# A three-layer block in split fp32: the other feature-major projections in wide and narrow matmuls, in two banks

## The chip, the core and the metric

The kernel runs on one core of a Trainium2 chip. The metric is the time of one execution in device microseconds (us); the median over runs counts. TensorE (PE) multiplies, ScalarE (ACT) and VectorE (DVE) work on the results and prepare the weights, GpSimd (POOL) does a few small things, and SyncE (SP) starts most of the transfers. Each engine works through its own queue in the order in which the program was written, and the engines wait for each other through semaphores.

## What is computed

The reference is a transformer of three layers on 256 tokens of width 1024, in fp32. The first block has a gated convolution, a stick-breaking attention with 16 heads, a cross attention and an MLP. The second block is a hybrid layer, run twice: eight heads of attention with a forget bias ("fox"), four heads of retention, and an MLP. The projections that the change touches are these:

```python
proj = h @ w_in[l]                                       # first block
c_h, c_b, c_c, sq, sk, sv, xq, gate_pre = jnp.split(proj, split_idx, axis=-1)
y_conv = (c_b * causal_depthwise_conv(c_c * c_h, conv_w[l])) @ w_conv_out[l]
...
proj = jnp.einsum('bsd,dc->bsc', x, w_in)                # second block, per layer
fq, fk, fv, f_logit, rq, rk, rv, rg = jnp.split(proj, SPLITS, axis=-1)
...
ret_out = jax.nn.silu(rg) * ret
```

sq, sk, c_h, c_c, c_b of the first block and fq, fk, rg of the second are wanted feature-major: features in the partitions, tokens along the free dimension.

## The kernel before

**Split products.** Every fp32 operand is held as two parts, a rounded "hi" and the rest "lo". A product is three matmuls: hi by hi, hi by lo and lo by hi (`mm3`, L324). The activations lie as `xT` (L440): a tile of 128 partitions by 8 feature blocks by 2 parts by 256 tokens, so that for one feature block the hi part and the lo part stand side by side in 512 columns.

**Weights.** The weights come in chunks of 128 x 2048 (`Stream`, L166), each in two pieces. For a piece SP starts a transfer of 512 KB, ACT rounds it to hi (L213) and DVE subtracts to get lo (L214). `W.pump(1)` issues one piece, and two where fewer than three chunks are ready ahead; five chunks have buffers. `tick()` (L283) is the clock of the program: it lets every generator in `sides` go on to its next `yield`, which issues that generator's work at this place of all queues, and then pumps the weights. So the order of work on each engine is written out by where the ticks stand.

**Feature-major chunks.** `stream_a` (L370) takes a chunk of 256 output features and one accumulator, a bank of PSUM with 512 fp32. Its left half takes features 0 to 127 for 256 tokens (24 matmuls of 256 columns), then comes a `tick()`, then the right half takes the other 128 features (24 more). It returns the accumulator, and the caller reads it there: `split` (L316) rounds on ACT and subtracts on DVE; `ch` is copied by ACT; `cc` and `cb` are multiplied by DVE; `rg` goes through Silu on ACT. There are 32 such chunks: five in each of the four passes of the loop at L554 (sq, sk, ch, cc, cb), and in each of the two layers of the second block fq, fk, fq, fk (L1133) and rg, rg (L1216).

`stream_w` (L352) is the other form, which the MLPs use before the change too (36 chunks): two accumulators, one for each half of the features. Sixteen matmuls of 512 columns take the hi weights by both parts of x side by side, then comes the `tick()`, and then 16 matmuls of 256 columns add the lo weights by the hi part. The two halves of an accumulator are then added by whoever evicts it; in the MLPs that is one DVE reduction.

**Accumulators.** `acc()` (L263) takes one of four banks. A bank is given back when its last reader stands in the program, and of the free ones the one given back longest ago is handed out (so the addresses in the program before go). A tile that gets a bank must wait until the readers of the tile before it have run. The other four banks serve `aux()` and `bank()`.

**The side work of the loop at L554.** `sb_pair` (L512) is started twice in each pass, after sk. By ticks, the first pair issues its scores (12 small matmuls into an `aux`, L516) at the tick inside cc; with them, at the same place, three activations on ACT (L522 to L524) and three operations on DVE (L525 to L527). At the tick after cc it issues an exponential on ACT (L530) and a mask product on DVE (L532). At the tick inside the next pass's sq it issues six transposes on PE and a copy `pt` on ACT (L541); and at the tick after the next sk its products with v (called PV here, 8 small matmuls into an `acc()`, L546) and their split into `osb`. The second pair does the same from the tick inside the next sq: scores there, transposes after ch, and PV at the tick inside cb.

**The side work in the layers.** During fq and fk, `csum_side` and `ret_qk_side` (L1037, L1052) each use an `acc()` at a time. `ret_side` (L1162) starts at the tick inside the first rg chunk: it takes one accumulator and then two (`ps`), whose group norm on DVE and POOL (L1185 to L1191) ends with `on`. All of that stands in the queues ahead of what follows that tick.

Of the kernel before, what the change touches and what calls it, by code (L numbers as in the profile page):

```python
# [9 lines left out]
F32 = mybir.dt.float32  # L10
F32R = mybir.dt.float32r
BF16 = mybir.dt.bfloat16
AF = mybir.ActivationFunctionType
ALU = mybir.AluOpType
# [3 lines left out]
S = 256  # L18
# [221 lines left out]
def block_kernel(ctx: ExitStack, tc: tile.TileContext, a: dict, out: bass.AP, upto=None, dbg=None):  # L240
    nc = tc.nc
    ctx.enter_context(tc.manual_schedule())

    def pool(stack, name, bufs=1, side="left", space=None):
        kw = {} if space is None else {"space": space}
        return stack.enter_context(tc.tile_pool(name=name, bufs=bufs, side=side, reuse_waits="tile", **kw))
# [16 lines left out]
    def acc():  # L263
        return accp.tile([128, 512], F32, tag="acc", name="acc")
# [9 lines left out]
    def bank():  # L274
        assert cur_ps[0][1] == 1
        return cur_ps[0][0].tile([128, 512], F32, tag="bank", name="bank")
# [3 lines left out]
    W = Stream(nc, rp, wp, a["wpack"])  # L280
    sides = []

    def tick(n=1):  # L283
        for g in list(sides):
            if next(g, "end") == "end":
                sides.remove(g)
        W.pump(n)
# [17 lines left out]
    def act_set(name):  # L305
        if cur_set[0] != name:
            nc.scalar.preload_act_table_set(name)
            cur_set[0] = name

    def tt(o, x, y, op):  # L310
        nc.vector.tensor_tensor(o, x, y, op=op)

    def stt(o, x, s, y, op0, op1):
        nc.vector.scalar_tensor_tensor(out=o, in0=x, scalar=s, in1=y, op0=op0, op1=op1)  # L314

    def split(hi, lo, src):  # L316
        nc.scalar.copy(hi, src)  # L317
        tt(lo, src, hi.bitcast(F32), ALU.subtract)

    def split_scaled(hi, lo, src, s):  # L320
        nc.scalar.mul(hi, src, s)
        stt(lo, src, s, hi.bitcast(F32), ALU.mult, ALU.subtract)

    def mm3(o, lh, ll, rh, rl, first, last):  # L324
        nc.tensor.matmul(o, lhsT=lh, rhs=rh, start=first, stop=False, skip_group_check=True)  # L325
        nc.tensor.matmul(o, lhsT=lh, rhs=rl, start=False, stop=False, skip_group_check=True)  # L326
        nc.tensor.matmul(o, lhsT=ll, rhs=rh, start=False, stop=last, skip_group_check=True)  # L327
# [9 lines left out]
    def mm(o, l, r, first=True, last=True):  # L337
        nc.tensor.matmul(o, lhsT=l, rhs=r, start=first, stop=last, skip_group_check=True)  # L338

    def unit_a(o, w, nt, x):  # L340
        for k in range(8):
            ns = slice(nt * 128, nt * 128 + 128)
            mm3(o, w[0][:, k, ns], w[1][:, k, ns], x[0][:, k, :], x[1][:, k, :], k == 0, k == 7)
# [8 lines left out]
    def stream_w(key, x, evict):  # L352

        w = W.get(key)
        ps = [acc(), acc()]
        for nt in range(2):
            for k in range(8):
                mm(ps[nt].rearrange("p (s t) -> p s t", s=2), w[0][:, k, nt * 128:nt * 128 + 128], x[2][:, k],  # L360
                   k == 0, False)
        tick()
        for nt in range(2):
            for k in range(8):
                mm(ps[nt][:, 0:S], w[1][:, k, nt * 128:nt * 128 + 128], x[0][:, k, :], False, k == 7)
            if nt:
                W.free()
            evict(nt, ps[nt].rearrange("p (s t) -> p t s", s=2))

    def stream_a(key, x):  # L370
        w = W.get(key)
        p = acc()
        pv = p.rearrange("p (n t) -> p n t", n=2)
        unit_a(pv[:, 0, :], w, 0, x)
        tick()
        unit_a(pv[:, 1, :], w, 1, x)
        W.free()
        return pv

    def stream_b(key, x, evict=None):  # L380

        p = [acc(), acc()]
        for j in range(2):
            w = W.get((*key, j))
            for t in range(2):
                unit_b(p[t], w, t, x, 4 * j, j == 0, j == 1)
                if t:
                    W.free()
                if j and evict is not None:
                    evict(t, p[t])  # L390
                if not (j and t):
                    tick()
        return p
# [46 lines left out]
    def new_xT():  # L440

        xT = ap.tile([128, 8, 2, S], F32R, tag="xT", name="xT")
        return xT[:, :, 0, :], xT[:, :, 1, :], xT


    hT = new_xT()
# [49 lines left out]
    sp = pool(st1, "sb", side="right")  # L496
# [55 lines left out]
        split(osb[0][:, pair, :], osb[1][:, pair, :], o[:, 0:256])  # L552

    for i in range(4):  # L554
        p = stream_a(("sq", i), hT)
        split_scaled(qs[0], qs[1], p, 0.125)
        tick()
        p = stream_a(("sk", i), hT)
        split(kb[0], kb[1], p)
        tick()  # L560
        sides.append(sb_pair(i, 0, 2, 3))
        sides.append(sb_pair(i, 1, 6, 4))
        p = stream_a(("ch", i), hT)
        chs = sp.tile([128, 2, S], F32, tag="chs", name="chs")
        nc.scalar.copy(chs, p)
        tick()
        p = stream_a(("cc", i), hT)
        tt(u[:, :, 2:], p, chs, ALU.mult)
        cv = sp.tile([128, 2, S], F32, tag="cv", name="cv")
        for nt in range(2):  # L570
            ct = 2 * i + nt
            nc.vector.tensor_scalar(cv[:, nt, :], u[:, nt, 0:S], cw[:, ct, 0:1], None, op0=ALU.mult)
            stt(cv[:, nt, :], u[:, nt, 1:S + 1], cw[:, ct, 1:2], cv[:, nt, :], ALU.mult, ALU.add)
            stt(cv[:, nt, :], u[:, nt, 2:S + 2], cw[:, ct, 2:3], cv[:, nt, :], ALU.mult, ALU.add)
        tick()
        p = stream_a(("cb", i), hT)
        tt(cv, p, cv, ALU.mult)
        split(yc[0][:, 2 * i:2 * i + 2, :], yc[1][:, 2 * i:2 * i + 2, :], cv)
        tick()
# [45 lines left out]
    for n in range(2):  # L625
# [4 lines left out]
        def evict(t, p):  # L630
            tt(sg[:, t, :], p, sg[:, t, :], ALU.mult)
            tt(merged[:, t, ns], merged[:, t, ns], sg[:, t, :], ALU.add)
# [90 lines left out]
    for h in range(2):  # L723
        box = {}
        p = stream_b(("xk", h), memT)
# [3 lines left out]
        p = stream_b(("xq", h), hT)  # L729
        box["qn"] = qk_prep(p, gq, "q")  # L730
        tick()
        p = stream_b(("xv", h), memT)
# [241 lines left out]
    xT = x2T[0]  # L974
    for l in range(2):
        st = ExitStack()
        p2 = pool(st, f"mix{l}")

        def T(shape, dt, tag, bufs=1):
            return p2.tile(shape, dt, tag=tag, name=tag, bufs=bufs)  # L980
# [23 lines left out]
        for t in range(2):  # L1004
            pk = bank()
            for i in range(2):
                p = bank()
# [68 lines left out]
        fp = pool(fst, f"fox{l}", side="right")  # L1076
# [54 lines left out]
            split(mix[0][:, pair, :], mix[1][:, pair, :], o[:, 0:256])  # L1131

        for i in range(2):  # L1133
            p = stream_a((l, "fq", i), xT)
            split_scaled(fqs[0], fqs[1], p, 0.125)
            tick()
            p = stream_a((l, "fk", i), xT)
            split(fkb[0], fkb[1], p)
            tick()
            for nt in range(2):  # L1140
                fox.append(fox_pair(i, nt, *((0, 1, 4, 9), (0, 4, 7, 10), (1, 3, 6, 8), (4, 6, 8, 10))[2 * i + nt]))
            sides.extend(fox[-2:])
# [70 lines left out]
        rgt = T([128, 4, S], F32, "rkT")  # L1213
        ret = ret_side()
        sides.append(ret)
        for i in range(2):  # L1216
            p = stream_a((l, "rg", i), xT)
            s = rgt[:, 2 * i:2 * i + 2, :]
            act_set(SILU)
            nc.scalar.activation(s, p, AF.Silu)  # L1220
            rgs[f"s{i}"] = s
            tick()
        nT = [None]
# [71 lines left out]
        xT = nT2[0]  # L1295
# [33 lines left out]
```

## Time and profile before

| | us |
|---|---|
| median of 3 runs (1205.63 to 1205.94) | 1205.88 |
| the profiled execution | 1206.04 |
| its span, first to last instruction | 1204.3 |

| engine | busy us | share of the span |
|---|---|---|
| PE | 1192.1 | 99% |
| DVE | 783.6 | 65% |
| ACT | 631.6 | 52% |

The profile is one execution, taken instruction by instruction. A busy share is an average over all stages. The chain of waits is followed back from the last instruction: at each step to what released it, or to the instruction before it on its engine. The timeline gives start and duration of each instruction in order of time. Matmuls overlap in the pipeline, so what one costs is the distance from its start to the start of the next, and not its duration. PEclk is the clock that TensorE was granted, as a share of 2.4 GHz. The forms x8, x12 and so on count instructions that one row holds.

### The profile page before, as it was taken

What the parts mean: (1) busy time and instruction counts of PE and PEld (TensorE: products, weight loads), DVE (VectorE), ACT (ScalarE), POOL (GpSimd) and SP (SyncE); (2) the same over time, 40 slices, a digit from 0 to 9 for tenths busy, and PEclk for the clock granted to TensorE, in tenths of its full rate; (3) what the DMA queues carried; (4) which work ended last, traced back from release to release, by engine and by line L of the source; (5) the groups of instructions that cost most, each with busy time, mean ns of one, the idle gap of its engine ahead of it and who ended that gap; (6) DMA issues with size and microseconds to landing.
All of it is one profiled execution on the core that took longest, in us unless ns stands there. A gap on an engine that the chain in (4) does not pass through costs nothing.

```text
span 1204.3 us, 17150 instructions
## 1 busy us (share of the span) xinstructions
PE 1192.1 (99%) x6801; PEld 1030.6 (86%) x6801; DVE 783.6 (65%) x1018; ACT 631.6 (52%) x885; POOL 27.1 (2%) x45
## 2 busy tenths in 40 slices
PE   8999999999999999999999999999999999999997
PEld 5999997888888888888898888888889888888886
DVE  6487776566665666566576686655667668665563
ACT  6455555455554566455255556645535555664550
POOL 1000000000000000000000100000000010000000
PEclk8999999999999999999999999999999999999999
DMA  8644456765455675555544366565545436656430
GB/s 324 236 134 140 148 176 194 250 194 173 143 163 187 192 241 193 210 174 206 169 163 143 120 218 224 182 222 173 195 153 185 140 126 217 219 186 228 162 136 35
DMA packets 60608, 218.92 MB, mean 182 GB/s; under 512 B 6864, under 2 KB 7264, under 8 KB 60528
## 3 DMA queue, kind: packets, MB, share of 16 engines
q1 hardware_dynamic: 58320, 210.99, 52.3%
q0 software_dynamic: 1776, 6.38, 1.6%
q8 instruction: 53, 0.87, 0.3%
q10 hardware_dynamic: 432, 0.46, 0.1%
q14 instruction: 27, 0.22, 0.1%
HBM read 216.75 MB, written 1.05 MB: 181 GB/s over the span
## 4 chain that ended last, share of the span: by engine, by line
PE 98%; DMA 1%; DVE 0%; POOLq 0%; issue 0%; ACT 0%; DVEq 0%; SPq 0%
PE acc L338 19%; PE bank L325 13%; PE bank L326 13%; PE bank L327 13%; PE acc L325 12%; PE acc L327 12%; PE acc L326 12%; PE acc L423 2%; PE aux L334 1%; DMA raw<-in_wpack_dram 1%; DMA gmix<-in_g_mix_dram 1%; PE aux L1119 0%; PE aux L539 0%; PE aux L326 0%; PE aux L327 0%; PE aux L325 0%
## 5 line engine op out<-in xcount | busy, mean ns | idle before, releaser
L214 DVE TENSOR_TENSOR wlo<-raw,whi 128x1024 fp32r<-128x1024 f32 x392 | 465.6, 1221 | 103.0 <-ACT whi L213 99.7
L213 ACT CAST whi<-raw 128x1024 fp32r<-128x1024 f32 x392 | 394.9, 1049 | 93.9 <-PE bank L327 41.3
L325 PE MATMUL bank<-whi,hid 128*128 128x512 f32 (+1 forms) x388 | 150.6, 388 | 0.5 <-DVE x L314 0.5
L326 PE MATMUL bank<-wlo,hid 128*128 128x512 f32 (+1 forms) x388 | 150.3, 387 | 0.0
L327 PE MATMUL bank<-whi,hid 128*128 128x512 f32 (+1 forms) x388 | 150.1, 387 | 0.0
L325 PE MATMUL acc<-xT,whi 128*128 128x256 f32 x512 | 147.6, 288 | 0.0
L326 PE MATMUL acc<-xT,whi 128*128 128x256 f32 x512 | 144.8, 283 | 0.0
L327 PE MATMUL acc<-xT,wlo 128*128 128x256 f32 x512 | 144.8, 283 | 0.0
L338 PE MATMUL acc<-xT,whi 128*128 128x512 f32 x576 | 136.9, 390 | 0.0
L338 PEld LDWEIGHTS acc<-xT,whi 128*128 128x128 f32 x576 | 107.0, 188 | 21.5
L826 ACT ACTIVATE r<-r 128x512 f32<-128x512 f32 x36 | 22.8, 633 | 148.3 <-DVE r L867 148.3
L325 PEld LDWEIGHTS acc<-xT,whi 128*128 128x128 f32 x512 | 98.0, 191 | 1.9 <-issue 1.0
L326 PEld LDWEIGHTS acc<-xT,whi 128*128 128x128 f32 x512 | 98.1, 192 | 0.2
L327 PEld LDWEIGHTS acc<-xT,wlo 128*128 128x128 f32 x512 | 98.0, 191 | 0.0
L325 PE MATMUL acc<-whi,xT 128*128 128x512 f32 x224 | 90.8, 405 | 0.3 <-ACT xT L317 0.2
L326 PE MATMUL acc<-wlo,xT 128*128 128x512 f32 x224 | 88.4, 395 | 0.5 <-DVE wlo L214 0.5
L327 PE MATMUL acc<-whi,xT 128*128 128x512 f32 x224 | 88.4, 395 | 0.0
L325 PEld LDWEIGHTS bank<-whi,hid 128*128 128x128 f32 x388 | 72.9, 188 | 15.0 <-DVE x L314 0.7
L327 PEld LDWEIGHTS bank<-whi,hid 128*128 128x128 f32 x388 | 72.9, 188 | 15.0
L326 PEld LDWEIGHTS bank<-wlo,hid 128*128 128x128 f32 x388 | 73.0, 188 | 14.1
L867 DVE TENSOR_REDUCE r<-acc 128x256 f32<-128x512 f32 x72 | 48.0, 688 | 50.9 <-PE acc L338 50.9
L338 PEld LDWEIGHTS acc<-xT,wlo 128*128 128x128 f32 x576 | 73.6, 191 | 2.6
(276 smaller groups left out, 1761.0 us busy)
## 6 DMA issues: line engine op xcount, KB each, us to landing
raw<-in_wpack_dram SPq DMA_DIRECT2D x388, 512.0 KB, 4.4
raw<-in_wpack_dram SPq DMA_DIRECT2D x4, 528.0 KB, 4.1
gb<-in_ln_g_dram POOLq DMA_DIRECT2D x4, 512.0 KB, 3.9
bb<-in_ln_b_dram POOLq DMA_DIRECT2D x4, 512.0 KB, 5.5
x<-in_x_dram SPq DMA_DIRECT2D x3, 512.0 KB, 5.7
mem<-in_mem_dram SPq DMA_DIRECT2D x2, 512.0 KB, 6.5
cst<-in_c_dram POOLq DMA_DIRECT2D x1, 898.0 KB, 9.1
out_dram<-x SPq DMA_DIRECT2D x3, 256.0 KB, 2.0
```

The costliest lines, as they stand in the source:

```text
L213: nc.scalar.copy(hi, raw)
L214: nc.vector.tensor_tensor(lo, raw, hi.bitcast(F32), op=ALU.subtract)
L325: nc.tensor.matmul(o, lhsT=lh, rhs=rh, start=first, stop=False, skip_group_check=True)
L326: nc.tensor.matmul(o, lhsT=lh, rhs=rl, start=False, stop=False, skip_group_check=True)
L327: nc.tensor.matmul(o, lhsT=ll, rhs=rh, start=False, stop=last, skip_group_check=True)
L334: nc.tensor.matmul(o[:, h, :], lhsT=q[a][hs[h]], rhs=k[b][hs[h]], start=i == 0, stop=i == 2, skip_group_check=True)
L338: nc.tensor.matmul(o, lhsT=l, rhs=r, start=first, stop=last, skip_group_check=True)
L423: nc.tensor.transpose(o[:, k * 128:(k + 1) * 128], src[:, k * 128:(k + 1) * 128], ident)
L826: nc.scalar.activation(dst, src, AF.Relu)
L867: lambda nt, h: nc.vector.tensor_reduce(rv[:, nt, :], h, AX.X, ALU.add))
```

## The change

`stream_a` goes. In its place `stream_s` computes the 32 chunks with `stream_w`, and evicts each of the two accumulators into a tile in SBUF: ACT copies the first half, and DVE adds the second half to that copy. The callers then read the SBUF tile in place of the accumulator. The new tiles are called `st` (two buffers); `ch` and `rg` are evicted straight into their own tiles, and the Silu of rg runs in place. The tick inside the chunk now stands after the 16 wide matmuls.

```diff
-    def stream_a(key, x):
-        w = W.get(key)
-        p = acc()
-        pv = p.rearrange("p (n t) -> p n t", n=2)
-        unit_a(pv[:, 0, :], w, 0, x)
-        tick()
-        unit_a(pv[:, 1, :], w, 1, x)
-        W.free()
-        return pv
+    def stream_s(key, x, dst):
+
+        def evict(nt, h):
+            nc.scalar.copy(dst[:, nt, :], h[:, :, 0])
+            tt(dst[:, nt, :], h[:, :, 1], dst[:, nt, :], ALU.add)
+
+        stream_w(key, x, evict)
+        return dst
...
-        p = stream_a(("sq", i), hT)
+        p = stream_s(("sq", i), hT, sp.tile([128, 2, S], F32, tag="st", name="st", bufs=2))
         split_scaled(qs[0], qs[1], p, 0.125)
...
-        p = stream_a(("ch", i), hT)
-        chs = sp.tile([128, 2, S], F32, tag="chs", name="chs")
-        nc.scalar.copy(chs, p)
+        chs = stream_s(("ch", i), hT, sp.tile([128, 2, S], F32, tag="chs", name="chs"))
...
-            p = stream_a((l, "rg", i), xT)
-            s = rgt[:, 2 * i:2 * i + 2, :]
+            s = stream_s((l, "rg", i), xT, rgt[:, 2 * i:2 * i + 2, :])
             act_set(SILU)
-            nc.scalar.activation(s, p, AF.Silu)
+            nc.scalar.activation(s, s, AF.Silu)
```

sk, cc, cb, fq and fk change as sq does. `stream_w`, which is not changed, is the function that it now calls:

```python
w = W.get(key)
ps = [acc(), acc()]
for nt in range(2):
    for k in range(8):
        mm(ps[nt].rearrange("p (s t) -> p s t", s=2), w[0][:, k, nt * 128:nt * 128 + 128], x[2][:, k], k == 0, False)
tick()
for nt in range(2):
    for k in range(8):
        mm(ps[nt][:, 0:S], w[1][:, k, nt * 128:nt * 128 + 128], x[0][:, k, :], False, k == 7)
    if nt:
        W.free()
    evict(nt, ps[nt].rearrange("p (s t) -> p t s", s=2))
```

## Rows read from the trace of the kernel before

**Rows 1.** Page, part 1: engine, busy us (share of span), instructions.
```profile
PE 1192.1 (99%) x6801; PEld 1030.6 (86%) x6801; DVE 783.6 (65%) x1018; ACT 631.6 (52%) x885; POOL 27.1 (2%) x45
```

**Rows 2.** Page, part 4: chain that ended last, by engine.
```profile
PE 98%; DMA 1%; DVE 0%; POOLq 0%; issue 0%; ACT 0%; DVEq 0%; SPq 0%
```

**Rows 3.** Waits of PE: waiter, releaser, us in total, times, longest.
```profile
PE acc L423 <- DVE ht L314: 2.2, 1, 2.2
PE acc L325 <- ACT xT L317: 0.2, 1, 0.2
```

**Rows 4.** Timeline of PE: start, duration in us, line, output<-inputs, shape.
```profile
37.02 0.28 PE L325 MATMUL acc<-xT,whi 128*128 128x256 f32 x1
57.26 0.51 PE L334 MATMUL aux<-kb,q 64*128 64x256 f32 x4
```

**Rows 5.** Chain in order of time (start, us, what), two MLP stretches.
```profile
447.41 1.92 PE acc L338 x16
460.24 11.11 PE acc L338 x64
```

**Rows 6.** The same chain, 56 to 160 us: scores of the attention pairs.
```profile
57.33 0.84 PE aux L334 x12
104.67 0.84 PE aux L334 x12
114.32 0.81 PE acc L338 x8
124.60 0.84 PE aux L334 x12
158.72 0.84 PE aux L334 x12
```

**Rows 7.** Timeline of ACT, third iteration of the head loop.
```profile
107.53 0.79 ACT L541 COPY pt<-aux 128x768 f32<-128x768 f32 x1
117.23 0.58 ACT L317 CAST kb<-acc 128x512 fp32r<-128x512 f32 x1
125.53 0.81 ACT L522 ACTIVATE e<-aux 128x768 f32<-128x768 f32 x1 [2.01 <-PE aux L334]
128.00 1.03 ACT L213 CAST whi<-raw 128x1024 fp32r<-128x1024 f32 x1
131.91 0.85 ACT L530 ACTIVATE r<-r 128x768 f32<-128x768 f32 x1 [2.87 <-DVE r L311]
133.59 0.36 ACT L317 CAST osbh<-acc 128x256 fp32r<-128x256 f32 x1
```

**Rows 8.** Timeline of DVE, the same iteration.
```profile
115.62 0.68 DVE L314 SCALAR_TENSOR_TENSOR q<-acc,q 128x512 fp32r<-128x512 f32 x1
119.09 0.68 DVE L311 TENSOR_TENSOR kb<-acc,kb 128x512 fp32r<-128x512 f32 x1
128.13 0.96 DVE L314 SCALAR_TENSOR_TENSOR e<-aux,e 128x768 f32<-128x768 f32 x1 [3.35 <-ACT e L524]
131.79 1.22 DVE L214 TENSOR_TENSOR wlo<-raw,whi 128x1024 fp32r<-128x1024 f32 x1
132.92 0.68 DVE L311 TENSOR_TENSOR u<-acc,chs 128x512 f32<-128x512 f32 x1
136.25 0.68 DVE L311 TENSOR_TENSOR r<-r,dmask 128x512 f32<-128x512 f32 x1
137.99 0.42 DVE L311 TENSOR_TENSOR osbl<-acc,osbh 128x256 fp32r<-128x256 f32 x1
139.46 0.68 DVE L311 TENSOR_TENSOR cv<-acc,cv 128x512 f32<-128x512 f32 x1
```

**Rows 9.** Timeline, first layer of the second block: PE, then DVE.
```profile
674.30 0.28 PE L325 MATMUL acc<-xT,whi 128*128 128x256 f32 x1
677.26 0.88 PE L338 MATMUL acc<-fpt,ta 128*64 128x256 f32 x8
682.27 0.36 PE L325 MATMUL acc<-xT,whi 128*128 128x256 f32 x1
692.73 0.48 PE L325 MATMUL bank<-whi,mixh 128*128 128x512 f32 x1
680.77 0.30 DVE L1185 BATCH_NORM_STATS2 gst<-acc 128x6 f32<-128x128 f32 x1 [1.74 <-PE acc L338]
688.17 1.37 DVE L1191 TENSOR_SCALAR on<-acc,gmv,grs 128x128 f32<-128x128 f32 x4 [1.13 <-POOL grs L419]
```

**Rows 10.** By stretch: start:end, length, busy us (count) PE to POOL, PEclk.
```profile
5.00:10.00 5.00, 2.77 (x13) 1.76 (x10) 2.10 (x5) 2.28 (x6) 0.55 (x1) 0.82 0.95 367
10.00:15.00 5.00, 4.97 (x11) 3.41 (x11) 4.33 (x6) 4.78 (x8) 1.67 (x3) 0.50 1.04 419
```

More of the change, by code (lines that the diff above doesn't have):

```diff
@@ L554, in block_kernel @@
     for i in range(4):
-        p = stream_a(("sq", i), hT)
+        p = stream_s(("sq", i), hT, sp.tile([128, 2, S], F32, tag="st", name="st", bufs=2))
         split_scaled(qs[0], qs[1], p, 0.125)
         tick()
-        p = stream_a(("sk", i), hT)
+        p = stream_s(("sk", i), hT, sp.tile([128, 2, S], F32, tag="st", name="st", bufs=2))
         split(kb[0], kb[1], p)
@@ L562, in block_kernel @@
         sides.append(sb_pair(i, 1, 6, 4))
-        p = stream_a(("ch", i), hT)
-        chs = sp.tile([128, 2, S], F32, tag="chs", name="chs")
-        nc.scalar.copy(chs, p)
+        chs = stream_s(("ch", i), hT, sp.tile([128, 2, S], F32, tag="chs", name="chs"))
         tick()
-        p = stream_a(("cc", i), hT)
+        p = stream_s(("cc", i), hT, sp.tile([128, 2, S], F32, tag="st", name="st", bufs=2))
         tt(u[:, :, 2:], p, chs, ALU.mult)
@@ L575, in block_kernel @@
         tick()
-        p = stream_a(("cb", i), hT)
+        p = stream_s(("cb", i), hT, sp.tile([128, 2, S], F32, tag="st", name="st", bufs=2))
         tt(cv, p, cv, ALU.mult)
@@ L1133, in block_kernel @@
         for i in range(2):
-            p = stream_a((l, "fq", i), xT)
+            p = stream_s((l, "fq", i), xT, fp.tile([128, 2, S], F32, tag="st", name="st", bufs=2))
             split_scaled(fqs[0], fqs[1], p, 0.125)
             tick()
-            p = stream_a((l, "fk", i), xT)
+            p = stream_s((l, "fk", i), xT, fp.tile([128, 2, S], F32, tag="st", name="st", bufs=2))
             split(fkb[0], fkb[1], p)
```

## The prediction

> **What bounds the kernel now.** Read the engines' shares first: PE is busy 99% of the span, DVE 65%, ACT 52% [rows 1]. The chain of waits says the same: PE holds 98% of it [rows 2]. PE's own waits confirm it: five in all, 4.6 us together, the longest 2.2 us and the shortest 0.2 us [rows 3]. So the time is the sum of PE's work, and each change of a matmul's cost shows in full, as long as PE still waits for nobody. Whether it does is read from the DVE and ACT timelines of the loop over heads, not from a share.
>
> **What the change gives on PE.** Before, from the first matmul of sq to the first scores lie 3.5 chunks, 168 matmuls of 256 columns, in 57.26 - 37.02 = 20.24 us [rows 4]: 0.1205 us each, 5.78 us per chunk of 48. The new form already runs in the MLPs: 64 matmuls, two whole chunks, take 11.11 us, so 5.555 per chunk, and 16 narrow ones 1.92, so the 16 wide ones take 3.63 [rows 5]. The columns are the same (48 x 256 = 16 x 512 + 16 x 256); a wide matmul only wastes less. The gain is 0.228 us per chunk, and 32 chunks give 7.3 us.
>
> **What it adds on ACT and DVE.** Per chunk two ACT copies and two DVE adds of 128x256 out of PSUM. The nearest rows have the same shape: the ACT cast takes 0.36 us [rows 7], the DVE subtraction 0.42 [rows 8]. The add can cost no less than half a 512-column operation (0.34) and no more than a whole one (0.68) [rows 8]; I take 0.42. On each of DVE's pairs that is some 0.75 us, 3.8 us per pass of five chunks; a pass is 158.72 - 124.60 = 34.12 us [rows 6], and DVE at 65% has room. Busy time is thus not the trouble. ch loses its one copy, a gain on ACT off the path. Weight pieces stay one per tick, at moved places; their transfers on SP's queue go out as the raw buffers come free, and three ready chunks (over 16 us) cover a slip. No step of POOL is passed, but retention's group norm comes 0.7 us later, as its tick does.
>
> **What it does to the banks.** Before, a chunk held one of four banks and its reader could be late by about three chunks. It is late. The cc chunk ends at 124.60 + 0.84 + 24 x 0.1205 = 128.3 [rows 4, 6], and DVE reads it at 132.92; sk ends at 114.32 and DVE reads it at 119.09; sq ends at 104.67 + 0.84 + 2.89 = 108.4, and DVE reads it at 115.62 [rows 6, 8]: 4.6 to 7.2 us, while the next chunk runs. It costs nothing because four banks allow it. Now a chunk holds two, and PV takes one between. Banks go to whoever asks next, the one given back longest ago first. That gives, in a steady pass: PV inside cb gets cc's first bank; sq gets cc's second and PV's; sk gets cb's two; PV after sk gets sq's first; ch gets sq's second and sk's first; cc gets sk's second and PV's. So PE needs an eviction a chunk or less after it was issued, and it stands in DVE's queue behind the side work of the tick inside the chunk.
>
> I walk one pass down the three queues; time 0 is the end of cc's scores. ACT runs three activations; DVE starts at 2.7 (128.13 against 125.44), its three operations take 3.66, the weight piece 1.13 [rows 7, 8]: cc's first add ends at 7.9, its second at 8.25. Then u and the convolution take 3.33 (132.92 to 136.25), the mask 0.6, a piece [rows 8]: 13.4.
> - PE: cc's narrow matmuls to 1.92, cb's wide ones to 5.55. PV needs cc's first bank, 7.9: **wait 2.35**. PV (0.81 [rows 6]) to 8.8, cb ends at 10.7, sq's first 8 wide to 12.5. Its second bank is PV's, which DVE's split leaves at 13.4 + 0.42 = 13.8: **wait 1.3**. Wide done 15.6, transposes and scores (0.84 each [rows 6]) to 17.3.
> - DVE: a piece, cb's adds to 15.55, cv 16.3; ACT casts it, DVE subtracts (17.6), ACT takes a piece (17.9), `pt` (0.7 to the next start), and only then the scores' activations, to 21.1. DVE's score work to 24.8, the piece to 25.9, sq's adds to 26.3 and 26.65.
> - PE: sq ends at 19.2, sk at 24.75; PV needs sq's first bank: **wait 1.6**, to 27.2; ch's first 8 wide to 29.0. Its second bank is sk's first: q needs a cast (0.58) and 0.68 on DVE, 28.0; exponential (0.85) and mask, 28.7; two pieces, 31.3; the add 31.65 [rows 7, 8]. **Wait 2.7**. ch ends at 35.4, transposes 36.3, cc's wide 39.9, scores 40.8.
>
> So a pass takes 40.8 us against 34.12: the waits are 7.95, the gain in five chunks 1.14. DVE and ACT are idle again at the end of it, so it repeats. From the first pass to the second (67.27 - 34.12 = 33.15 before [rows 6]) there is no PV in cb; the same walk gives waits of 0.45, 0.7, 4.45 (PV after sk) and 2.8, and 40.4 us. Until the first scores nothing changes (the wide matmuls stand before the tick, which eats the gain so far). After the last scores the wait of 2.35 stays, less the gain, with later gates hiding the rest: +0.9. Stage: 7.3 + 6.7 + 6.7 + 0.9 = **+21.6 us**.
>
> In each layer the same walk over fq and fk gives small waits (about 0.4 and 0.5 us) that eat the four chunks' gain: +0.1. At rg the banks decide again: the second rg chunk gets the two `ps` banks, where `stream_a` got another. PE: rg from 674.30, wide to 677.93, side work 677.26 to 682.27 before, so 5.0 us, to 682.95, narrow 684.85. The group norm runs 680.77 to 688.17 + 1.37 and moves by 0.67: its first bank is free at 685.9, its second at 690.2 [rows 9]. Waits 1.1 and 2.4 us; PV, transposes and the rest end at 695.6 in place of 692.73: +2.9. Two layers: **+6.0 us**.
>
> **Sum.** 21.6 + 6.0 = 27.6 us. The profiled execution took 1206.04 us (span 1204.3), 0.16 over the median of 1205.88, so the two are one here: 1233.6, said as 1234.
>
> **Price of the unknown.** With the add at 0.34 the four waits of a pass shrink by some 0.1 each, with 0.68 they grow by 0.3 to 0.6: -1.5 to +6 us in all. ACT's copies wait in front of the adds only where ACT is last (sk): -1 to +2. The walk itself, with semaphores at nothing to 0.1 us each, I trust to 6 us. So 1222 to 1243 for this case.
>
> **The rivals.**
> - *Nobody waits, faster.* One mechanism: ACT and DVE evict within one chunk (5.55 us) at all those places, because the two engines run only 52% and 65%, and PE keeps its 7.3 us: 1206.04 - 7.3 = 1198.7. It decides at 5.5 us: below, no wait. Against it stand the lags of 4.6 to 7.2 us [rows 6, 8], and that score work, 3.66 + 1.13 us, stands ahead of the add by the program. The Trainium skill, "Perfetto Trace Analysis", Matmuls, speaks for it: independent groups should rotate through PSUM banks, so that evacuating one overlaps the matmuls of the next. This kernel rotated so before; by that rule two of four banks would do, and 1198.7 be right; the rows of the lags speak against it. Chance 0.06.
> - *Only some waits.* Where each wait lets DVE catch up more than I walk, the 2.35 us of PV in cb (three times) and the rg waits stay: 1206.04 - 7.3 + 7.05 + 2 x 3.5 = 1212.8. Chance 0.11.
> - *PE's clock falls.* At the start PE waits 2.2 us [rows 3] after 13 matmuls, and the granted clock goes from 2.4 to 1.2 GHz: mean 0.82 from 5 to 10 us, 0.50 from 10 to 15 [rows 10], together 6.8 us at the low level, 3.4 us lost. My walk has nine waits of 2.3 to 4.45 us (two per pass, one in the last, one per layer). If each costs up to 3.4, that is up to 30 us; a fall before a later wait is partly absorbed by it, so half: +15, 1249. Against it: between those waits PE works for 3 us or more each time, at full clock as far as the rows of before show it. The Trainium skill, "TensorE: Matmul & The Clock Gate", "A second HAM failure mode: psum-queue depth-cycling", tells of a kernel whose PE idled briefly between groups as it cycled through banks, and whose clock went up and down; before the change this trace shows no such thing after the first 15 us. Chance 0.27, since the one wait of that length that the trace has was followed by a fall.
>
> **Numbers.** Forecast as walked 0.52; clock falls 0.27; only some waits 0.11; nobody waits 0.06; gain and waits just cancel 0.04. What a measurement here tells from no change is 0.2%, 2.4 us. Faster 0.06, same 0.04, slower 0.90. The range takes in the forecast's own, the partial case and most of the clock's: 1211 to 1254, which leaves out some 0.17.
>
> **What would show it.** Right: PE busy falls below 97% in the stretch from 58 to 190 us, with waits on DVE's L311 (the adds) of 1 to 4.5 us at the first matmuls of PV, sq, sk and ch; scores of the first pair about 41 us apart; the wide matmuls 0.227 us apart; the MLPs as they were. In each layer two waits on L1191 at the second rg chunk. Wrong: PE without waits in that stretch, or passes of 33 us; a PEclk below 1.00 there would mean the clock's case; waits on weights (L213, L214) would mean that the pieces have slipped, which I cost at nothing.

## The result and the profile after

The changed kernel takes 1237.78 us (median of 4, 1237.52 to 1240.78) against 1205.86 for the kernel before on the same chip: ratio 1.0271, 95% interval 1.026 to 1.0283, 32 us slower. The forecast was 1234 with a range of 1211 to 1254. The profiled execution took 1237.97 us, with a span of 1236.2; against the 1206.04 of before that is +31.9, where the sum of the prediction was +27.6.

Part 1 of the page, then the first line of part 4 (the chain that ended last, by engine), answer to [rows 1, 2]:

```profile
PE 1196.3 (97%) x6289; PEld 1004.4 (81%) x6289; DVE 807.9 (65%) x1082; ACT 650.7 (53%) x945; POOL 27.0 (2%) x45
```

```profile
PE 87%; DVE 7%; ACT 3%; issue 2%; DMA 1%; POOL 0%; POOLq 0%; SPq 0%; DVEq 0%; ACTq 0%
```

DVE's share is the same 65% as before, and yet the chain now runs through DVE and ACT for a tenth of the span. A share does not show an engine that is late. PE's waits do (waiter, releaser, us in total, times, longest); before they were [rows 3]:

```profile
PE acc L338 <- DVE st L311: 19.5, 10, 4.3
PE acc L338 <- DVE on L1188: 6.0, 4, 2.2
PE acc L338 <- DVE osbl L311: 2.1, 2, 1.0
PE acc L422 <- DVE ht L314: 1.5, 1, 1.5
```

The first line is the adds of the new form, the second the group norm beside rg, the third the bank of the products with v (PV). The last one is at the start of the kernel and was there before.

The same scores as in [rows 6], in the chain of after (start, us, what). The passes take 40.55, 40.95 and 40.95 us in place of 33.15, 34.12 and 34.12:

```profile
57.20 0.85 PE aux L334 x12
97.75 0.85 PE aux L334 x12
138.70 0.85 PE aux L334 x12
179.65 0.85 PE aux L334 x12
```

All of PE's waits from the first scores to the end of the second pass, out of PE's timeline (the idle time before an instruction, and who ended it, stands in brackets):

```profile
65.94 3.96 PE L338 MATMUL acc<-xT,whi 128*128 128x512 f32 x16 [0.24 <-DVE st L311]
70.33 0.88 PE L538 MATMUL aux<-ident,r 128*128 128x128 f32 x6 [0.43 <-DVE r L311]
84.00 1.10 PE L338 MATMUL acc<-pt,v 128*64 128x256 f32 x8 [4.28 <-DVE st L311]
89.39 2.11 PE L338 MATMUL acc<-xT,whi 128*128 128x512 f32 x8 [0.92 <-DVE st L311]
106.56 0.88 PE L338 MATMUL acc<-pt,v 128*64 128x256 f32 x8 [2.22 <-DVE st L311]
112.42 2.11 PE L338 MATMUL acc<-xT,whi 128*128 128x512 f32 x8 [1.04 <-DVE osbl L311]
124.96 0.88 PE L338 MATMUL acc<-pt,v 128*64 128x256 f32 x8 [1.27 <-DVE st L311]
130.35 2.11 PE L338 MATMUL acc<-xT,whi 128*128 128x512 f32 x8 [2.48 <-DVE st L311]
```

The four from 106.56 on are the steady pass, and they come again 41 us later (147.51, 153.37, 165.90, 171.29). What stands ahead of the add that PV waits for at 106.56 is seen in DVE's timeline: a score operation and a piece of the weights, then cc's two adds, the first of which ends at about 106.5.

```profile
104.07 0.96 DVE L311 TENSOR_TENSOR r<-aux,r 128x768 f32<-128x768 f32 x1
104.95 1.22 DVE L214 TENSOR_TENSOR wlo<-raw,whi 128x1024 fp32r<-128x1024 f32 x1
106.08 0.75 DVE L311 TENSOR_TENSOR st<-acc,st 128x256 f32<-128x256 f32 x2
```

In the layers the two waits stand at the second rg chunk:

```profile
708.31 2.11 PE L338 MATMUL acc<-xT,whi 128*128 128x512 f32 x8 [0.79 <-DVE on L1188]
712.62 3.64 PE L338 MATMUL acc<-xT,whi 128*128 128x512 f32 x8 [2.20 <-DVE on L1188]
```

The second row's eight wide matmuls take 3.64 us, those of the first 2.11. The granted clock says why. By stretch (start:end, length, busy us and count of PE to POOL, PEclk, DMA share, GB/s):

```profile
58.00:190.00 132.00, 109.95 (x676) 91.21 (x675) 97.36 (x131) 74.73 (x114) 0.00 (x0) 0.99 0.38 124
84.00:92.00 8.00, 7.07 (x30) 5.26 (x31) 6.14 (x10) 6.08 (x10) 0.00 (x0) 0.79 0.56 171
92.00:190.00 98.00, 81.83 (x516) 67.88 (x516) 71.17 (x96) 55.24 (x85) 0.00 (x0) 1.00 0.39 128
708.00:722.00 14.00, 11.49 (x58) 9.03 (x59) 8.61 (x22) 6.16 (x10) 2.10 (x3) 0.88 0.48 154
1015.00:1030.00 15.00, 12.64 (x63) 9.88 (x64) 9.28 (x24) 6.29 (x10) 2.09 (x3) 0.89 0.55 169
```

Before, the first of these stretches was:

```profile
58.00:190.00 132.00, 132.00 (x1061) 123.96 (x1060) 101.49 (x119) 79.66 (x101) 0.00 (x0) 1.00 0.47 149
```

PE, which was busy for the whole of the stretch from 58 to 190 us, is now busy for 83% of it. The clock fell three times: after the wait of 4.28 us, and once in each layer. Each time 0.12 x 14, 0.11 x 15 or 0.21 x 8, about 1.7 us, are lost, that is 3.4 us at 1.2 GHz. From 92 to 190 us it did not fall in this execution, though PE waited 2.2 to 2.5 us five times.

Where the 31.9 us are: at the end of the loop over heads the same chunk starts at 191.28 in place of 169.21, +22.1; each of the two layers adds 4.9 to 5.0. The rest of the kernel adds nothing. PE's timeline there, before and after:

```profile
169.21 0.40 PE L325 MATMUL acc<-whi,xT 128*128 128x512 f32 x1
191.28 0.40 PE L325 MATMUL acc<-whi,xT 128*128 128x512 f32 x1
```

### The profile page after: what moved, and what is told of

The parts are those of the page before. It is cut to its first block, busy times and chain, and to the rows that moved or that the text cites. A ratio compares the mean times of both kernels' runs of the same rounds, so it can differ in the third digit from the quotient of the medians.

```text
span 1236.2 us, 16222 instructions
## 1 busy us (share of the span) xinstructions
PE 1196.3 (97%) x6289; PEld 1004.4 (81%) x6289; DVE 807.9 (65%) x1082; ACT 650.7 (53%) x945; POOL 27.0 (2%) x45
## 4 chain that ended last, share of the span: by engine, by line
PE 87%; DVE 7%; ACT 3%; issue 2%; DMA 1%; POOL 0%; POOLq 0%; SPq 0%; DVEq 0%; ACTq 0%
PE acc L338 25%; PE bank L325 12%; PE bank L327 12%; PE bank L326 12%; PE acc L325 7%; PE acc L326 7%; PE acc L327 7%; DVE wlo L214 2%; PE acc L422 2%; DVE r L525 1%; PE aux L334 1%; DVE st L311 1%; DVE e L314 1%; DMA raw<-in_wpack_dram 1%; ACT whi L213 0%
## 5 line engine op out<-in xcount | busy, mean ns | idle before, releaser
L338 PE MATMUL acc<-xT,whi 128*128 128x512 f32 x1088 | 267.3, 397 | 14.3 <-DVE st L311 6.1
L338 PEld LDWEIGHTS acc<-xT,whi 128*128 128x128 f32 x1088 | 203.5, 191 | 60.1 <-DVE st L311 8.6
L338 PEld LDWEIGHTS acc<-xT,wlo 128*128 128x128 f32 x1088 | 137.7, 191 | 4.7 <-issue 0.5
L311 DVE TENSOR_TENSOR hid<-r,hid 128x512 fp32r<-128x512 f32 x36 | 24.9, 692 | 72.7 <-ACT hid L317 72.7
L325 PE MATMUL bank<-whi,xT 128*128 128x512 f32 (+2 forms) x192 | 68.7, 358 | 0.0
L327 PE MATMUL bank<-whi,xT 128*128 128x512 f32 (+2 forms) x192 | 68.0, 354 | 0.0
L326 PE MATMUL bank<-wlo,xT 128*128 128x512 f32 (+2 forms) x192 | 68.0, 354 | 0.0
L325 PEld LDWEIGHTS acc<-whi,xT 128*128 128x128 f32 x224 | 42.7, 191 | 10.9 <-ACT xT L317 1.0
```

## The experiments

Two theories stood at the start. *Banks*: a chunk that holds two of four accumulators, given back by a DVE that is late, makes PE wait. *Load*: the added copies and adds make ACT and DVE late for work that PE needs. A third came up on the way, *the tie*: ACT, which before waited for PE alone, now waits for DVE, and what stands behind it in ACT's queue gets late too.

### One place at a time

e1_loop has the new form in the loop over heads only, e2_layers in the two layers only.

```diff
-            p = stream_s((l, "fq", i), xT, fp.tile([128, 2, S], F32, tag="st", name="st", bufs=2))
+            p = stream_a((l, "fq", i), xT)
...
-            s = stream_s((l, "rg", i), xT, rgt[:, 2 * i:2 * i + 2, :])
+            p = stream_a((l, "rg", i), xT)
```

> The new form only in the 20 chunks of the loop over heads; the 12 chunks of the two layers as before. Theory (the waits for banks in the loop cost 7.95 us a pass): the loop ends 21 to 23 us later and the rest is as before, so 1227 to 1229, with the twelve waits of the changed kernel up to 190 us and none on the group norm. Rival (each changed chunk costs the same, some 1 us, whatever stands around it): 20 of 32 chunks, so 1206 + 20 = 1226 and waits spread evenly over the chunks; the next run tells these two apart better.

> The new form only in the 12 chunks of the two layers; the loop over heads as before. Theory: 5 us in each layer, all of it at the second rg chunk (waits of 0.8 and 2.2 us and a stretch of matmuls at the low clock behind them), so 1215 to 1217. With the run before it adds up to the changed kernel's +32. Rival (the same cost for each changed chunk): 12 of 32, 1218, lying in fq and fk as much as in rg.

Measured: e1_loop 1229.75 us, ratio 1.0198 (1.0183 to 1.0213); e2_layers 1214.21, ratio 1.0073 (1.0058 to 1.0088). Against the 1205.67 of before in the same job that is +24.1 and +8.5, together 32.6 for the 32 of the whole change: the two places do not help or hurt each other. Both medians lie 0.8 us outside what was expected, e1_loop above and e2_layers below. The first of PE's waits in e1_loop:

```profile
PE acc L338 <- DVE st L311: 18.4, 9, 4.3
```

And in e2_layers:

```profile
PE acc L338 <- DVE on L1200: 6.0, 4, 2.2
```

e2_layers waits at the second rg chunk only; fq and fk, with the same copies and adds, let PE wait for none of them.

The loop is the same in e1_loop and in the changed kernel, and so are the five waits of 2.2 to 2.5 us after 92 us. But in e1_loop's profiled execution the clock fell behind two of them, 2.22 us before PV at 106.51 and 2.47 us at 130.30. Two stretches of the changed kernel, and then the same two of e1_loop (the last three numbers are PEclk, DMA share and GB/s):

```profile
104.00:112.00 8.00, 5.16 (x34) 3.84 (x32) 7.75 (x15) 3.74 (x6) 0.00 (x0) 1.00 0.22 67
128.00:136.00 8.00, 5.65 (x35) 5.12 (x36) 6.68 (x10) 5.52 (x11) 0.00 (x0) 1.00 0.53 177
104.00:112.00 8.00, 5.78 (x31) 4.64 (x30) 7.75 (x14) 3.84 (x6) 0.00 (x0) 0.79 0.20 67
128.00:136.00 8.00, 5.70 (x27) 4.96 (x28) 6.39 (x9) 4.23 (x9) 0.00 (x0) 0.79 0.50 176
```

The pass from 106.51 to the next PV inside cb, at 149.03, took 42.52 us there, against 40.95 in the changed kernel. So whether a fall follows is not settled by the length of the wait alone.

### The added work alone, and the tie

e7_load_free is the kernel before with two more ACT copies and two more DVE adds per chunk at the places where the change puts them, between SBUF tiles, with nobody waiting for them.

```diff
+        for nt in range(2):
+            nc.scalar.copy(ex[:, nt, :], x[0][:, nt, :].bitcast(F32))
+            tt(ey[:, nt, :], x[0][:, nt, :].bitcast(F32), x[1][:, nt, :].bitcast(F32), ALU.add)
         return pv
```

> The kernel before with two ACT copies and two DVE adds of 128x256 behind each of the 32 chunks, as in the load run before it, but now they read tiles that have long been in SBUF and nobody waits for them: no bank is held, no queue is tied to the other. Theory (work alone costs little): 1206 to 1211; the transposes inside sq have 1.1 us of slack behind the mask on DVE, and the adds of one chunk take 0.75. In the earlier load run ACT's second copy waited for DVE's add of the first, since both halves lay in one bank; that tie, not the work, would then be its +34. Rival (the work): 1225 or more here too.

Measured: 1206.36 us, ratio 1.0006 (0.9997 to 1.0015), at DVE 67% and ACT 54%. The work alone is free.

e4_load adds the same operations, but reads them out of the accumulator, one bank with both halves.

```diff
+        for nt in range(2):
+            nc.scalar.copy(ex[:, nt, :], pv[:, nt, :])
+            tt(ex[:, nt, :], pv[:, nt, :], ex[:, nt, :], ALU.add)
         return pv
```

> The kernel before with the work of the eviction added and nothing else: behind each of the 32 chunks two ACT copies of 128x256 out of the accumulator into a tile that nobody uses, and two DVE adds to them. The matmuls and the banks are as before. Theory (added work costs nothing while four banks allow a late reader): 1205 to 1208, PE without new waits over 0.5 us. Rival (the added 24 us on DVE and 21 us on ACT are what costs): 1225 or more, with waits on the same places as in the changed kernel.

Measured: 1239.62 us, ratio 1.0279 (1.0261 to 1.0296). The expectation was wrong by 32 us, and not because of the load. The largest wait of ACT that e4_load adds, in the view of ACT's waits:

```profile
ACT st L382 <- DVE st L311: 80.2, 32, 5.2
```

And the first line of PE's waits in e4_load:

```profile
PE aux L546 <- DVE r L311: 14.9, 4, 5.5
```

ACT's copy of the second half waits for DVE's add of the first, 32 times, though they read different columns: both lie in one bank. The SBUF tile that both write is not what ties them. In the changed kernel the two halves lie in two banks and go to one SBUF tile just so, and there ACT copies both halves of cc one after the other, some 4 us before DVE's adds of them start at 106.08 (ACT's timeline):

```profile
102.10 0.64 ACT L373 COPY st<-acc 128x256 f32<-128x256 f32 x2
```

The Trainium skill, "PSUM — Partial Sum Buffer", PSUM bank collisions raise a hardware error, says that the compiler's back end adds a dependency between any two instructions on different engines that touch the same bank and the same 32 partitions, reads as well as writes. This trace agrees, with 32 such waits in 32 chunks. So ACT stands behind DVE, the activations of the scores start late, DVE gets its score work late, and PE's transposes wait for the mask, three times by 4.1 to 5.5 us.

e8_dep ties the engines in another way, with the matmuls and the banks of before: DVE copies each accumulator to SBUF, and the callers read the copy. ACT's casts then wait for DVE.

```diff
-        return pv
+        ex = extra[0].tile([128, 2, S], F32, tag="st", name="st", bufs=2)
+        nc.vector.tensor_copy(ex, pv)
+        return ex
```

> The kernel before with one thing more: DVE copies each of the 32 accumulators to SBUF in one instruction (0.68 us), and the callers read that copy. Matmuls and banks as before. So ACT's casts of q, k and yc and the Silu, which waited for PE alone, now wait for DVE's turn. Theory (a part of the loss is ACT, which works in order, standing behind DVE's late eviction): slower, 1209 to 1220, PE waiting at the transposes for the mask. If the banks are all of it: 1205 to 1207.

Measured: 1227.01 us, ratio 1.0176 (1.0162 to 1.0189), more than expected. No accumulator keeps PE waiting in the loop; four transposes do (PE's waits in e8_dep):

```profile
PE aux L544 <- DVE r L311: 9.9, 4, 4.1
```

DVE is busy for 805.5 us there and for 803.7 in e7_load_free, so it is not the amount of work. A tie of ACT to DVE is thus dear by itself. Whether it is what makes the changed kernel slow had to be told apart from the banks.

### Half after half, one bank at a time

e3_halves keeps the wide and narrow matmuls and the eviction, but finishes the first 128 features in one accumulator (8 wide, 8 narrow), evicts it, comes to the tick, and then does the other half.

```diff
+        for nt in range(2):
+            p = acc()
...
+            nc.scalar.copy(dst[:, nt, :], p[:, 0:S])
+            tt(dst[:, nt, :], p[:, S:2 * S], dst[:, nt, :], ALU.add)
+            if nt == 0:
+                tick()
```

> All 32 chunks with the same matmuls, the same ACT copies and the same DVE adds as in the changed kernel, but one half after the other: one accumulator takes its 8 wide and its 8 narrow matmuls and is evicted before the second half asks for its own, and the tick stands between the halves. A chunk holds one bank at a time. Theory (the wait is for the bank): a half asks for the bank of the fourth tile before it, some 9 us back, where DVE is 8 us late; the waits go but for some 0.1 us each, and the 7.3 us that wide matmuls save remain: 1198 to 1202. Rival (the added work on ACT and DVE is what PE waits for): the work is the same, so 1230 or more. Second rival (the order wide, then narrow is slow in itself at these places): 1230 or more without waits.

Measured: 1220.18 us, ratio 1.012 (1.0105 to 1.0135). More than half of the loss is gone, but not all, and the 1198 to 1202 of the theory are far: three waits of 2.9 to 3.0 us are left, one in each pass but the first, all at ch's first half (PE's timeline of e3_halves):

```profile
121.11 2.92 PE L338 MATMUL acc<-xT,whi 128*128 128x512 f32 x8 [2.98 <-DVE st L311]
```

It needs the bank of sq's second half, whose add stands behind the score work. The clock falls after each (mean 0.91 from 120 to 140 us). ACT's casts still wait for DVE's adds in this kernel (those of q for 12.7 us in four waits), which neither the theory nor a rival provided for.

e9_scores_later moves DVE's three score operations of e3_halves one tick later, to let that add pass.

```diff
+        yield
         stt(e3, zz, 0.0, e3, ALU.max, ALU.add)
...
-        for _ in range(gap):
+        for _ in range(gap - 1):
             yield
```

> The kernel with one bank at a time (half after half), and the three DVE operations on the scores issued one tick later than the three ACT activations they wait for, so that DVE takes the weight piece and the second half's eviction first. Theory (the 3 us that PE waits in each pass for sq's second half is DVE standing in its queue for ACT's activations): the three waits go, with them the stretches of low clock behind them, 1199 to 1206. Rival (DVE has too much work in the loop in any order, 30.5 of 33 us): 1215 or more.

Measured: 1225.96 us, ratio 1.0169 (1.0155 to 1.0183), slower than e3_halves. PE's waits for an accumulator's add shrink from 8.8 us to 2.9, as the theory has it, but the time does not. The mask goes later with the scores, and PE's transposes wait for it four times, 2.3 to 3.0 us. What DVE is given first, the other side waits for.

### ACT straight from the first half

e11_direct is the changed kernel with its two accumulators per chunk, but ACT rounds q, k, fq and fk from the first half in PSUM, where it stands anyway, and waits for PE alone again; DVE's subtraction takes the sum.

```diff
+            nc.scalar.copy(dst[:, nt, :], h[:, :, 0])
+            if s is None:
+                nc.scalar.copy(hi[:, nt, :], h[:, :, 0])
+            else:
+                nc.scalar.mul(hi[:, nt, :], h[:, :, 0], s)
+            tt(dst[:, nt, :], h[:, :, 1], dst[:, nt, :], ALU.add)
```

> The changed kernel, with two accumulators per chunk as it has them, but ACT rounds q, k, fq and fk to their hi part straight from the first half in PSUM, next to its copy of that half, and no longer from the tile that DVE has added to; DVE's subtraction then takes the whole sum. So ACT waits for PE alone at those places, as before the change. If banks given back late are the main cause (the walk of the prediction), PV inside cb still waits about 2.2 us for cc's first bank, and the second sq half about 1 us, since these stand behind DVE's score work and not behind a cast: the two waits at ch's second half and at PV after sk shrink by the cast and its round trip, 0.6 to 1.3 us each, and the time is 1228 to 1235. If the main cause is that ACT's queue stands behind DVE's additions, nearly all waits go and the time is 1210 to 1218.

Measured: 1233.62 us, ratio 1.0228 (1.0212 to 1.0244). The second pass in PE's timeline of e11_direct:

```profile
105.77 0.88 PE L338 MATMUL acc<-pt,v 128*64 128x256 f32 x8 [2.21 <-DVE st L311]
111.63 2.11 PE L338 MATMUL acc<-xT,whi 128*128 128x512 f32 x8 [1.03 <-DVE osbl L311]
124.25 0.88 PE L338 MATMUL acc<-pt,v 128*64 128x256 f32 x8 [1.36 <-DVE st L311]
128.43 2.11 PE L338 MATMUL acc<-xT,whi 128*128 128x512 f32 x8 [1.26 <-DVE st L311]
```

Three of the four waits stand as in the changed kernel; only that of ch's second half falls, from 2.48 to 1.26. The tie through the casts is worth 4.2 us of the 32.

### Taking one user out of the ring

The next kernels join the two: half after half, ACT rounding from PSUM, and rg in its form of before. e12_halves_direct and e13_late_fq also give PV of the even pairs a place in the other four banks, so that it stands no longer in the ring of four accumulators (the last two pairs of the loop had such a place before, so three PVs move); e14_pv_acc is e13_late_fq without that. In e12_halves_direct ACT rounds fq's first half ahead of the tick at which the heads of the chunk before still read fq, so their scores are formed of mixed operands, which is not what the reference computes; e13_late_fq and e14_pv_acc round it behind the tick.

```diff
-        o = acc() if pair < 6 else aux()
+        o = acc() if pair % 2 and pair < 6 else aux()
```

> Wide matmuls and then narrow ones for one half of the features in one accumulator, then the tick, then the other half in another one (one bank at a time, as before the change); ACT rounds q, k, fq and fk straight from the first half in PSUM; rg keeps its form of before; the products with v of the even pairs take a bank of the other four. If the two causes found so far (two banks held per chunk, and ACT standing behind DVE's additions) are all there is, PE waits for nobody for more than 0.5 us and keeps the gain of 28 chunks by 0.228 us, 6.4 us: 1199 to 1202, faster than both kernels. If the eviction that DVE owes is late by itself, wherever its operand stands, waits of 2 to 3 us stay at the second halves, and the time is 1212 or more.

> As the run before (halves one bank at a time, q, k, fq and fk rounded straight from PSUM), but at fq ACT's rounding of the first half and DVE's addition stand after the tick, since the heads of the chunk before still read fq at that tick. The loop over heads is the same, so it should again be 1.0 us shorter than in the kernel before; in the layers the first half's bank is held for half a chunk longer, which four banks allow: 1203.5 to 1205. If the bank time at fq does decide, the layers lose 1 us or more each: 1206 or more.

> As the other kernel of this pair, but the products with v of the even pairs take one of the four accumulators again, as in the kernel before and in the changed one; nothing else differs. If ACT standing behind DVE's additions was what made the form with one bank per half slow (1220.2), the fifth user of a bank changes little: 1204 to 1206. If the number of banks still decides, the products with v or the half after them wait 1 to 2.5 us in each of four passes for an addition that stands behind DVE's score work: 1208 to 1214.

Measured: e12_halves_direct 1204.18 us, ratio 0.9987 (0.9978 to 0.9996); e13_late_fq 1203.48, 0.9981 (0.9972 to 0.999); e14_pv_acc 1217.23, 1.0094 (1.008 to 1.0108). One user of a bank, three times in the loop, makes 13.7 us. PE's waits for an accumulator's add are, in e13_late_fq:

```profile
PE acc L338 <- DVE st L311: 0.6, 2, 0.3
```

And in e14_pv_acc:

```profile
PE acc L338 <- DVE st L311: 9.7, 3, 3.3
```

The second of these three in e14_pv_acc's timeline, DVE and then PE:

```profile
121.63 0.42 DVE L311 TENSOR_TENSOR st<-acc,st 128x256 f32<-128x256 f32 x1
122.10 2.25 PE L338 MATMUL acc<-xT,whi 128*128 128x512 f32 x5 [3.32 <-DVE st L311]
```

(The second row ends with the window that was asked for, at 125 us.)

DVE adds sq's second half from 121.63 us, and ch's first half starts at once. PE had finished that half of sq at 112.2, so DVE is 9.4 us late. In e13_late_fq it is just as late (107.8 and 117.20, behind the same score work), but the bank is asked for half a chunk later, by ch's second half, and PE waits 0.32 us. My expectation of e14_pv_acc, 1208 to 1214 if the banks decide, was too low, for the clock as in the changed kernel: three waits of 3.1 to 3.3 us make 9.7, within what was expected of four, and the clock, 1.00 in e13_late_fq from 57 to 200 us, has a mean of 0.96 over 82 us of that and of 0.97 over 61, which is up to 0.04 x 82 + 0.03 x 61 = 5 us more.

e13_late_fq is faster than the kernel before, by 2.2 us, at the edge of what can be told. It has 28 of the 32 chunks in the new form, which by the prediction's 0.228 us would give 6.4. So the 1199 to 1202 expected of e12_halves_direct did not come, although the waits of the loop went.

### The clock in the layers

e10_fill is e2_layers with nine matmuls of 512 columns, of which nothing is used, ahead of the second half of the second rg chunk: PE works there in place of waiting.

```diff
+                for _ in range(fill):
+                    mm(f[:, 0:512].rearrange("p (s t) -> p s t", s=2), x[0][:, 0, 0:128], x[2][:, 0])
```

> The kernel with the new form in the layers alone, with nine idle matmuls of 512 columns (2.0 us, into a bank that nobody reads) put where PE waits 2.2 us in the second rg chunk. Theory (a fall of the granted clock behind the wait, 3.4 us at half, costs some 1.7 us in each layer): the clock stays at 2.4 GHz and the time falls by 2 to 3.4 us, to 1211 to 1212. Rival (the clock costs nothing there, because DVE sets the pace): no change, 1214.

Measured: 1212.67 us, ratio 1.0057 (1.0043 to 1.0071), 1.5 below e2_layers. The stretch from 690 to 720 us in e2_layers, with a granted clock of 0.94:

```profile
690.00:720.00 30.00, 29.78 (x144) 24.29 (x145) 22.98 (x36) 16.59 (x23) 0.57 (x1) 0.94 0.56 188
```

And in e10_fill, at 1.00:

```profile
690.00:720.00 30.00, 29.82 (x151) 24.74 (x151) 24.43 (x38) 16.41 (x23) 0.57 (x1) 1.00 0.61 200
```

The chunk's second half starts at the same time in both (690.22 and 690.33), and what follows is quicker at full clock. From the start of rg in the first layer to its start in the second, e2_layers' profiled execution takes 306.89 us (674.18 to 981.07) and that of e10_fill 305.30 (674.28 to 979.58): with a fall a layer is 1.6 us longer. Between the medians it is 0.8 us per layer; the profiled execution of e2_layers was the slowest of its four, by 1.3 us. That the other three had fewer falls would explain it, but is not shown. All four times of e10_fill (1212.50 to 1212.69) lie below all four of e2_layers (1213.91 to 1215.77).

## Why the prediction was right, and what it missed

**What bounds the kernel.** Right, and so was the way of reading: DVE's 65% says nothing of lags of 4.6 to 7.2 us [rows 6, 8], and these decided. The shares hardly moved.

**The gain on PE.** The size is right, its arrival was not. In the changed kernel eight wide matmuls that follow each other without a wait take 1.84 and 1.81 us (117.96, 119.80, 121.61), so 16 take 3.65, against 3.63 in [rows 5]. But of 1.14 us per pass only 34.12 + 7.01 - 40.95 = 0.18 is seen. A wait seems to cost more than its idle time: the 16 wide ones ahead of PV start at 100.52, and the idle time before 106.56 begins at 104.34, 3.82 us later in place of 3.65, since idle time is counted from the end of the last one's record, an end that the profile models, and a wide matmul's own record lasts 0.40 us on the mean where the distance to the next start is 0.227. Four waits by some 0.17 to 0.2 us make 0.7 to 0.8 of the missing 0.96. In e13_late_fq, which has no such waits to speak of, a pass takes 33.93 us (90.26 to 124.19), also just 0.2 less than before; its one wait of 0.32 us costs 0.47, two halves cost 5.58, and the rest lies in the starts around the side work, which I have not taken apart.

**ACT's and DVE's costs.** Right: a lone add takes 0.42 us, a copy 0.36 to 0.38. *Busy time is thus not the trouble* is what e7_load_free shows. But e4_load shows that the same operations cost 34 us when a shared bank ties ACT to DVE; that step of the working had no such case. In the changed kernel DVE adds to what ACT has copied out of the same bank, so DVE follows ACT there anyway and this tie adds no wait.

**The walk of a pass.** Right at each place. Predicted waits of 2.35, 1.3, 1.6 and 2.7 us were 2.22, 1.04, 1.27 and 2.48; a pass of 40.8 was 40.95. The waits came out 0.94 shorter in sum, and the gain that failed to arrive, 0.96, makes up for it: that the two misses cancel is luck. The first pass was to take 40.4 and took 40.55, with 4.28 for the walked 4.45 at PV after sk. The stage was +22.1 for +21.6. That the banks are the cause, not only that the waits stand there, is shown by e14_pv_acc against e13_late_fq, where one user of a bank makes the waits come and go, and by e11_direct, which takes the casts out of DVE's way and leaves three of the four waits as they were. The first pair has one bank per half; the changed kernel itself with PV elsewhere was not run. *Price of the unknown* gave ACT's side little, and 4.2 us is what it came to.

**The layers.** The step that failed in size. The waits at the second rg chunk were predicted at 1.1 and 2.4 us and were 0.79 and 2.20, the eight places of fq and fk cost nothing to speak of, as said. But a layer is 4.95 us longer, not 3.0: the clock fell behind the wait of 2.20 in both layers, which the forecast's own case left out. With 1.65 us each in this execution, these two falls are 3.3 of the 4.3 us by which the sum was short.

**The rivals.** *Nobody waits* and *only some waits* did not come: eight of the nine walked waits of over 2 us are there, none spared by the one before it, and the ninth shrank for another reason. For *PE's clock falls* I took half of 3.4 us for nine waits. The changed kernel's trace shows three falls of 1.7 us. The one in the loop was swallowed by the next wait, as the rival's text allows: that is the ninth, 0.92 us where I had walked 2.8. That there were no more is in part luck, since e1_loop, with the same waits in the loop, had two more. The Trainium skill, "TensorE: Matmul & The Clock Gate", A second HAM failure mode: psum-queue depth-cycling, describes such falls where PE idles briefly between groups; the trace agrees after 4.28 us and in the layers, and differs from 92 to 190 us, where five idle times of 2.2 to 2.5 us between groups left the clock at 1.00; e1_loop's trace agrees at two of the same five. The Trainium skill, "Perfetto Trace Analysis", Matmuls, advises to rotate independent groups through the banks. Here it turned on how late the reader is: with the same DVE 9.4 us late, four banks were enough for e13_late_fq and too few for e14_pv_acc.

**What stays open.** What decides whether a wait of 2.2 to 2.5 us is followed by a fall of the clock: in the changed kernel one followed both of those at rg and none of five in the loop, in e1_loop two of the same five. And how much of e3_halves' 14.5 us is the tie and how much the ring: the direct casts alone (with rg in its old form) give 3.0, and PV's bank with them 16.7, but PV's bank without the direct casts was not tried.

## What to carry to other kernels

Before a chunk is given a second accumulator, write down who hands each bank back and how late that engine is at that place, from the timeline and not from its share; two of four banks with a reader 4.6 to 7.2 us late, in chunks of 5.6 us, made the kernel 32 us slower where 7.3 were to be gained. Where an engine's eviction must wait, keep the other engines' evictions off it: work that nobody waits for was free, and about as much work that tied ACT to DVE through one bank or one copied tile cost 34 and 21 us. When a ring is too small, look for the one user that can take a bank elsewhere.

## What the runs showed of the hardware that I had not expected

- ACT waits for DVE where both only read one bank, at different columns: 80.2 us in 32 waits in e4_load. With the halves in two banks and one SBUF tile, it did not.
- The granted clock fell to 1.2 GHz for about 3.4 us after waits of 4.28 us and of 2.20 us (at rg, behind one of 0.79), and did not after five of 2.2 to 2.5 in the loop. In e1_loop it fell after two of the same five, of 2.22 and 2.47 us.
- Idle time of PE by the profile seems to leave out some 0.17 us of what a wait costs: a 512-column matmul's record lasts 0.40 us, the next one starts after 0.227 where nothing waits.
